# Five edits in a two-block transformer kernel: a 31-tap convolution from ScalarE and GpSimd to TensorE, row sums inverted small, heads in banks of one kind, the scan's two sums in one bank, and the inverse moved ahead

## The chip, the cores and the metric

The kernel runs on one core of one Trainium2 chip. The metric is the device time of one execution in microseconds (us). The engines go by the names of the profile: PE (TensorE), DVE (VectorE), ACT (ScalarE), POOL (GpSimd), SP (the queue that issues most weight DMAs). L12 is line 12 of the kernel before.

## What is computed

Two chained blocks, each of two layers, for 256 tokens of width 1024 in float32 (block one also carries 256 context tokens, so its even layer works on 512). Block one, layer 0: a bidirectional gated delta-rule scan (GDN, 8 heads of 64, chunks of 64 tokens) beside a latent attention (MLA, 8 heads). Layer 1: neighbourhood attention (NA) beside grouped attention (GQA), 8 heads each. Block two, in both layers: an attention over the 256 best keys of an indexer, a 31-tap depthwise convolution and a pooling, side by side. After each mixer stands an FFN. The parts that are changed:

```
# delta rule, one chunk                          # softmax attention
v_new = u - w @ s                                p = exp(s - max);  o = (p @ v) / sum(p)
o     = q_dec @ s + qk @ v_new                   # block two, convolution branch
s     = s * g_last + k_dec^T @ v_new             c[t] = sum_j y[t - 30 + j] * dw[j] + b   (31 taps)
u, w  from the inverse of (I + m), 64 x 64       z = layer_norm(c) -> silu -> @ pw
```

## The kernel before

All matmuls with weights are written as three products of parts (`mm3`, L549 to L551): the weight is cut into a high part (ACT cast, L270) and a low rest (a subtraction on DVE, in some stretches on POOL, L272), the activation likewise (`split`, L306 and L307). Weights come in tiles of 128 rows by up to 1024 columns over SP's queue. The program is recorded through a scheduler that orders the instructions of each engine by itself; the source order and the pools decide what it may choose from. PSUM has eight banks of 128x512 float32; `bank(K, kind)` takes the next of a kind, and the kinds are shared out per stage (in layer 0: "g" 3, "s" 2, "tp", "po", "gv" one each, and "aux" means "g" there; elsewhere there are two "s", two "acc", two "tp").

*Layer 0* (`l0_mixer`): the in-projections with a 5-tap convolution as products with diagonal matrices (`gdn_conv`: ACT makes a diagonal from the identity in L882, PE multiplies by it in L886); `gdn_norm` and `gdn_matrices` (L1040 multiplies chunks 64x64); `gdn_blocks`, an elimination of 31 steps on DVE (L1086, L1088); `gdn_invert`, which turns its result (L1105) and multiplies 32x32 blocks (L1115, L1128); then the scan `gdn_run`, whose step is `gdn_state`: L1188 gives w @ s in one half of the partitions and q_dec @ s in the other, L1195 gives the update of s, L1206 the product qk @ v_new, and `gdn_o` adds each of the last two sums to the output. `l0_mla` fills the gaps of the scan. `mod_chunk` makes the modulation (L372 to L400) from its own weights; chunks 4 and 5 are gates.

*Attention* (`attend`, and `s_attend` in block two): scores in two banks for two heads, maximum (L669), exponential with its sum (L671), transposes (L674), copies (L677, L679), p @ v (L685). The inverse sums come from `sums_row`: a reciprocal that DVE takes of the sum repeated over 64 columns of each head (L693), and a product with the identity that turns them (L695); `attended` multiplies (L713, L714).

*Block two* (`s_mixer`): in-projection weights, 1872 columns; the indexer's scores (L1596 on) and its selection of 256 keys (L1603 to L1623, DVE, with MAX8 and MATCH_REPLACE8); the convolution (`conv`): for each of 2 x 128 channels and each of 30 further taps

```
            nc.scalar.mul(m, yp[:, c, j:j + 256], dw[:, i, c, j:j + 1])
            nc.gpsimd.tensor_tensor(o, o, m, op=ALU.add)
```

(L1516 and L1517), its transposes (L1531), and its layer norm in `finish`; then `att(1)`, `att(0)` (scores L1638 and L1642, transposes L1653, copies L1654, p @ v L1659), and the out-projection.

## Time and profile before

| | us |
|---|---|
| median of 3 runs | 2181.03 (2169.08 to 2183.77) |
| the profiled execution | 2178.34, of it the span of the trace 2176.6 |
| PE busy | 1992.6 (92% of the span) |
| DVE / ACT / POOL busy | 1382.2 / 931.8 / 370.7 |
| mean granted clock of PE | 0.917 of full speed |

A busy PE is not a PE at full speed: its clock has two levels, 1.2 and 2.4 GHz, shown as 0.50 and 1.00. A stretch is therefore read by two numbers, how much of it PE was busy and at what clock.

### The profile page before, as it was taken

The numbers are of one execution on the slowest core, as the hardware profiler recorded it, in microseconds if no ns is written. First come the engines' busy times: TensorE is split into PE (matmuls) and PEld (weight loads), VectorE is DVE, ScalarE is ACT, GpSimd is POOL, SyncE is SP. The second block draws the span as 40 slices with busy tenths as digits, with TensorE's granted clock in tenths as the row PEclk, the third lists the DMA queues.
The fourth block names the chain that finished last, engine by engine and source line by source line (L and its number), as shares of the span: only waits on it lengthen the run. The fifth ranks groups of instructions, "written<-read, shape, count | busy, mean of one in ns | idle before, by whom it ended". The sixth has DMA issues, their size and how long they took to land.

```text
span 2176.6 us, 30043 instructions
## 1 busy us (share of the span) xinstructions
PE 1992.6 (92%) x11008; PEld 1585.0 (73%) x11008; DVE 1382.2 (64%) x2699; ACT 931.8 (43%) x1612; POOL 370.7 (17%) x454
## 2 busy tenths in 40 slices
PE   6989799898999999899879998988899998879998
PEld 4778578678878778676557887865688787558886
DVE  5665557767776744638575555785765568666644
ACT  4533443344222234444454443753554357345532
POOL 2211112301000000213130002641200057040000
PEclk9999799899999999999788999966999999579999
DMA  8344540233676632223044573513556443055652
GB/s 279 90 112 122 190 131 26 67 98 111 191 259 215 189 106 93 90 68 97 20 145 141 164 230 100 145 54 113 168 175 195 153 113 109 29 164 166 191 186 68
DMA packets 186947, 291.82 MB, mean 134 GB/s; under 512 B 28472, under 2 KB 75704, under 8 KB 186800
## 3 DMA queue, kind: packets, MB, share of 16 engines
q1 hardware_dynamic: 172720, 272.54, 40.2%
q0 software_dynamic: 5472, 16.13, 2.3%
q10 hardware_dynamic: 8608, 1.23, 0.4%
q8 instruction: 87, 1.43, 0.3%
q14 instruction: 60, 0.49, 0.1%
HBM read 281.44 MB, written 8.41 MB: 133 GB/s over the span
## 4 chain that ended last, share of the span: by engine, by line
PE 75%; DVE 13%; DMA 5%; ACT 4%; issue 2%; POOL 1%; SPq 0%; ACTq 0%; DVEq 0%; POOLq 0%
PE acc L549 17%; PE acc L550 17%; PE acc L551 17%; DVE wlo L272 2%; DMA wraw<-in_w_in_dram 2%; PE s L549 2%; PE s L550 2%; PE s L551 2%; PE po L685 2%; PE tp L886 2%; DMA wraw<-in_w_mod_dram 1%; PE gv L372 1%; ACT whi L270 1%; PE tp L674 1%; PE s L1642 1%
## 5 line engine op out<-in xcount | busy, mean ns | idle before, releaser
L272 DVE TENSOR_TENSOR wlo<-wraw,whi 128x512 fp32r<-128x512 f32 (+4 forms) x748 | 488.7, 697 | 292.4 <-ACT whi L270 276.5
L270 ACT CAST whi<-wraw 128x1024 fp32r<-128x1024 f32 (+4 forms) x420 | 413.4, 989 | 456.1 <-PE acc L551 180.9
L549 PE MATMUL acc<-whi,u 128*128 128x512 f32 (+3 forms) x1320 | 512.5, 391 | 28.3 <-ACT u L306 15.9
L550 PE MATMUL acc<-wlo,u 128*128 128x512 f32 (+3 forms) x1320 | 511.7, 389 | 4.4 <-DVE wlo L272 4.4
L551 PE MATMUL acc<-whi,u 128*128 128x512 f32 (+3 forms) x1320 | 510.3, 388 | 0.8 <-DVE u L307 0.7
L549 PEld LDWEIGHTS acc<-whi,u 128*128 128x128 f32 x1320 | 254.3, 193 | 80.9 <-ACT u L306 18.2
L550 PEld LDWEIGHTS acc<-wlo,u 128*128 128x128 f32 x1320 | 254.3, 193 | 55.2 <-DVE wlo L272 8.0
L551 PEld LDWEIGHTS acc<-whi,u 128*128 128x128 f32 x1320 | 253.2, 192 | 52.3 <-DVE u L307 4.3
L272 POOL TENSOR_TENSOR wlo<-wraw,whi 128x512 fp32r<-128x512 f32 (+1 forms) x92 | 115.1, 1280 | 400.5 <-ACT whi L270 400.4
L549 PE MATMUL acc<-u,whi 128*128 128x512 f32 (+1 forms) x480 | 174.1, 369 | 5.0 <-ACT u L1558 2.7
L550 PE MATMUL acc<-u,whi 128*128 128x512 f32 (+1 forms) x480 | 174.0, 364 | 2.4 <-DVE u L307 2.4
L551 PE MATMUL acc<-u,wlo 128*128 128x512 f32 (+1 forms) x480 | 173.1, 365 | 2.2 <-DVE wlo L272 2.2
L1517 POOL TENSOR_TENSOR u<-u,cvm 128x256 f32<-128x256 f32 x120 | 100.3, 836 | 64.2 <-ACT cvm L1516 55.8
L549 PEld LDWEIGHTS acc<-u,whi 128*128 128x128 f32 x480 | 93.9, 197 | 21.6 <-ACT u L1558 3.1
L431 DVE SCALAR_TENSOR_TENSOR msum<-mraw,u,msum 128x512 f32<-128x512 f32 x140 | 100.8, 746 | 13.4 <-DMA mraw<-in_w_mod_dram 12.4
L550 PEld LDWEIGHTS acc<-u,whi 128*128 128x128 f32 x480 | 94.5, 197 | 17.7 <-DVE u L307 3.1
L551 PEld LDWEIGHTS acc<-u,wlo 128*128 128x128 f32 x480 | 94.1, 197 | 17.6 <-DVE wlo L272 2.8
L307 DVE TENSOR_TENSOR u<-aux,u 128x512 fp32r<-128x512 f32 (+2 forms) x92 | 56.8, 629 | 34.8 <-ACT u L306 34.4
L306 ACT CAST u<-aux 128x512 fp32r<-128x512 f32 (+2 forms) x92 | 48.5, 541 | 59.2 <-PE aux L724 25.9
L549 PE MATMUL acc<-whi,dxh 128*128 128x512 f32 x176 | 69.7, 396 | 1.9 <-ACT dxh L306 1.9
L550 PE MATMUL acc<-wlo,dxh 128*128 128x512 f32 x176 | 69.6, 395 | 0.0
L551 PE MATMUL acc<-whi,dxl 128*128 128x512 f32 x176 | 69.0, 396 | 0.0
(501 smaller groups left out, 3037.8 us busy)
## 6 DMA issues: line engine op xcount, KB each, us to landing
wraw<-in_w_up_dram SPq DMA_DIRECT2D x64, 512.0 KB, 3.9
wraw<-in_w_down_dram SPq DMA_DIRECT2D x64, 512.0 KB, 4.2
mraw<-in_w_mod_dram SPq DMA_DIRECT2D x56, 512.0 KB, 4.9
wraw<-in_w_ffn_down_dram SPq DMA_DIRECT2D x44, 512.0 KB, 3.7
wraw<-in_w_mod_dram SPq DMA_DIRECT2D x40, 512.0 KB, 5.4
wraw<-in_w_ffn_gate_dram SPq DMA_DIRECT2D x48, 256.0 KB, 3.5
wraw<-in_w_ffn_up_dram SPq DMA_DIRECT2D x48, 256.0 KB, 3.9
wraw<-in_w_ffn_gate_dram SPq DMA_DIRECT2D x20, 512.0 KB, 3.8
```

Source lines behind the costliest of these rows:

```text
L270: self.K.nc.scalar.copy(hi, raw)
L272: e.tensor_tensor(lo[:, k], raw[:, k], hi.bitcast(F32)[:, k], op=ALU.subtract)
L306: (hi_eng or nc.scalar.copy)(hi, src)
L307: nc.vector.tensor_tensor(lo, src, hi.bitcast(F32), op=ALU.subtract)
L372: nc.tensor.matmul(ps[32 * j:32 * j + 32, :], K.cl[:, g + k, :], raw[:, k, :], start=(g + k < 4), stop=(g + k >= 4))
L431: nc.vector.scalar_tensor_tensor(accs[s], raw[:, k, :], c, accs[s], op0=ALU.mult, op1=ALU.add)
L549: mm(ps, ah, bh, start=start, stop=False)
L550: mm(ps, ah, bl, start=False, stop=False)
L551: mm(ps, al, bh, start=False, stop=stop)
L685: nc.tensor.matmul(po[hh * 64:hh * 64 + 64, c:c + 128], v(hh, j), pts[hh][0][:, j * 128:(j + 1) * 128], start=(j == 0), stop=(j == nj - 1))
L886: nc.tensor.matmul(tp[:, t * 128:(t + 1) * 128], x[:, t // 2, t % 2 * 128 + j:t % 2 * 128 + j + 128], dg[j], start=(j == 0), stop=(j == 4))
L1517: nc.gpsimd.tensor_tensor(o, o, m, op=ALU.add)
```

## The change

1. **Convolution.** The 240 ACT and POOL instructions of both layers go. ACT now makes a 128x128 diagonal per tap (`taps`, 32 per half of the channels, the 32nd being the bias against a tile of ones), and PE multiplies the shifted input by it, 64 products into each of the banks "po" and "tp" per layer and half of the channels taken together, so that the sum over taps is formed in PSUM. The transposes of L1531 go; `finish` reads the two banks.
2. **Sums.** `sums_row` goes. A reciprocal is taken of the sums alone (2 or 4 columns), and `normed` spreads four pairs at once (one DVE copy of 128x512), turns them with four products, copies and multiplies.
3. **Banks.** In layer 1, pairs take ("s","s","tp","tp") and ("acc","acc","tp","tp") in turn; in block two the second group of heads takes "acc". The transposes kept in `late` are recorded ahead of `na(1)`.
4. **Scan.** L1188 becomes two products of 64 columns; the q_dec @ s half stays open, and qk @ v_new is added to it in the same bank. One `gdn_o` per step instead of two, one bank less.
5. **Order in layer 0.** `gdn_invert` stands right behind `gdn_blocks`; `gdn_norm(0)` and `gdn_matrices(True)` stand ahead of the second convolution group and the gate projection; modulation chunks 4 and 5 stand in the middle of `l0_mla`.

```
-def sums_row(K, sm, rb, c):
-    n = sm.shape[1]
-    r = cut(K, [128, n, 2, 64], F32, "rs%d" % n, 2)
-    K.nc.vector.reciprocal(r, bc(sm, [128, n, 2, 64], 3))
-    for x in range(n):
-        K.nc.tensor.matmul(rb[:, c + x * 128:c + x * 128 + 128], r[:, x]..., K.ident, ...
+def normed(K, y, po, R, kind):
+    rb = bank(K, kind)
+    w = cut(K, [128, 512], F32, "pt", K.np)
+    K.nc.vector.tensor_copy(w..., bc(R.rearrange("p x h -> p (x h)"), [128, 8, 64], 2))
+    for x in range(4):
+        K.nc.tensor.matmul(rb[:, x * 128:x * 128 + 128], w[:, x * 128:x * 128 + 128], K.ident, ...
+    K.nc.scalar.copy(y, rb)
+    K.nc.vector.tensor_tensor(y, po, y, op=ALU.mult)
...
-            nc.tensor.matmul(ps[:, p * 128:(p + 1) * 128], wq[:, p, 2 * a:2 * a + 2, :]..., S[:, p, :], start=True, stop=True)
+            nc.tensor.matmul(ps[r, c], wq[:, p, 3 * a, :], S[:, p, :], start=True, stop=True)
+            nc.tensor.matmul(ps[o, c], wq[:, p, 1 + a, :], S[:, p, :], start=(p == 0), stop=False)
...
-        nc.tensor.matmul(po[o, hs], Q[r, h, :], vn[r, hs], start=True, stop=True)
-    if not first:
-        gdn_o(K, t, a, o, ps)
+        nc.tensor.matmul(po[o, hs], Q[r, h, :], vn[r, hs], start=first, stop=first or h == 7)
     gdn_o(K, t, a, o, po)
...
+    def taps(c):
+        for j in range(32):
+            if j % 3 == 0:
+                dg = cut(K, [128, 3, 128], F32, "dg", 2)
+            nc.scalar.mul(dg[:, j % 3, :], K.ident, dw[:, i, c, j:j + 1] if j < 31 else dwb[:, i, c:c + 1])
+            yield j, dg[:, j % 3, :]
+    def conv():
+        ps = [bank(K, "po"), bank(K, "tp")]
+        for c in range(2):
+            for j, dg in taps(c):
+                for t in range(2):
+                    nc.tensor.matmul(ps[t][:, c * 128:c * 128 + 128],
+                                     yp[:, c, t * 128 + j:t * 128 + j + 128] if j < 31 else ones, dg, ...
+        return ps
...
-    pss = [bank(K, "s") for _ in range(2)]
+    pss = [bank(K, "acc" if g else "s") for _ in range(2)]
...
-                        LX = gdn_blocks(K, Om)
+                        gdn_invert(K, *gdn_blocks(K, Om))
...
+                        gdn_norm(K, 0)
+                        gdn_matrices(K, True)
+                        with On(K, pg):
                             gdn_conv(K, W, 8, 4, False, True)
                             gdn_gate(K, W)
-                        gdn_norm(K, 0)
-                        gdn_matrices(K, True)
```

What the scheduler makes of it is seen in PE's order. Layer 0, before: the products of the inverse (L1115, L1128) stand behind the last pieces of `gdn_matrices` (L1040) and between modulation products (L372), with the scan's first products (L1154) next.

```order
L1040 MATMUL g_1901<-gT_1899,gT_1892 64x64 x8
L1040 MATMUL g_1902<-gT_1899,gT_1892 64x64 x8
L1115 MATMUL g_2013<-b_2009,u_144 32x32 x32
L1115 MATMUL g_2048<-b_2009,u_144 32x32 x32
L372 MATMUL gv_3272<-wraw_3273,u_124 32x512 x2
L372 MATMUL gv_3272<-wraw_3277,u_124 32x512 x2
L1128 MATMUL g_2083<-u_144,b_2010 32x32 x32
```

Layer 0, now (these lines are L1121 and L1134, `gdn_matrices` is L1034 and L1046):

```order
L1034 MATMUL tp_1796<-const_id_75,u_138 128x128 x4
L1121 MATMUL g_1136<-b_1132,u_144 32x32
L1121 MATMUL g_1171<-b_1132,u_144 32x32
L1121 MATMUL g_1136<-b_1132,u_144 32x32 x31
L1121 MATMUL g_1171<-b_1132,u_144 32x32 x31
L1134 MATMUL g_1206<-u_144,b_1133 32x32 x32
L1034 MATMUL tp_1803<-const_id_75,u_137 128x128
```

The inverse stands between the pieces of `gdn_matrices` now (row 591 of PE's order, where it stood at 750); the second convolution group and the gate projection follow it, and the scan's first state comes at row 798.

Block two, first layer, behind the last product of the in-projection; before: the indexer's products (L549 to L551 into "s") and turned queries (L1345), then the attention scores (L1638).

```order
L549 MATMUL s_12879<-u_12042,u_12120 128x128
L550 MATMUL s_12879<-u_12043,u_12120 128x128
L551 MATMUL s_12879<-u_12042,u_12121 128x128
L1345 MATMUL aux_12607<-const_id_75,akd_12593 128x128 x2
L1345 MATMUL aux_12612<-const_id_75,u_11693 128x128 x4
L1638 LDWEIGHTS u_11664
L1638 MATMUL s_12984<-u_11697,u_11664 128x256
```

Now (L1352 was L1345, L1648 was L1638, L1534 is the new product of the convolution):

```order
L550 MATMUL s_12868<-u_12064,u_12092 128x128
L551 MATMUL s_12868<-u_12063,u_12093 128x128
L1352 MATMUL aux_12616<-const_id_75,akd_12606 128x128 x2
L549 MATMUL s_12868<-u_12063,u_12099 128x128
L1534 MATMUL po_12640<-dg_12672,u_11719 128x128
L1534 MATMUL tp_12641<-dg_12672,u_11719 128x128
```

The convolution's products come in groups of up to twelve (two tiles of three diagonals) between the indexer's products and the attention scores: 10 of the layer's 128 stand ahead of the last product of the in-projection, 118 behind it, and the last of them ahead of the first p @ v.

## Rows read from the trace of the kernel before

**Rows 1.** The page: busy time, share of the span and instructions of each engine; PE's granted clock in tenths in 40 slices of 54.4 us; and the chain that ended last, by engine.

```profile
PE 1992.6 (92%) x11008; PEld 1585.0 (73%) x11008; DVE 1382.2 (64%) x2699; ACT 931.8 (43%) x1612; POOL 370.7 (17%) x454
...
PEclk9999799899999999999788999966999999579999
...
PE 75%; DVE 13%; DMA 5%; ACT 4%; issue 2%; POOL 1%; SPq 0%; ACTq 0%; DVEq 0%; POOLq 0%
```

**Rows 2.** Layer 0, stretches of time: start and end, length, busy time (and instructions) of PE, its weight loads, DVE, ACT and POOL, granted clock of PE, share of the DMA engines, GB/s.

```profile
142.00:200.00 58.00, 58.00 (x363) 49.94 (x365) 45.21 (x91) 20.62 (x45) 2.56 (x2) 1.00 0.26 73
200.00:220.00 20.00, 18.04 (x102) 14.05 (x94) 5.62 (x6) 5.93 (x11) 4.43 (x4) 1.00 0.59 123
220.00:240.00 20.00, 12.85 (x175) 6.54 (x174) 6.32 (x15) 4.91 (x9) 3.34 (x5) 0.83 0.66 208
240.00:260.00 20.00, 16.68 (x416) 10.88 (x414) 15.46 (x69) 10.88 (x29) 5.33 (x21) 0.57 0.64 217
260.00:280.00 20.00, 19.36 (x270) 16.09 (x267) 10.18 (x28) 9.41 (x17) 1.39 (x3) 0.66 0.34 108
280.00:390.00 110.00, 105.03 (x1194) 83.22 (x1192) 72.92 (x128) 44.08 (x104) 21.31 (x30) 1.00 0.24 75
```

**Rows 3.** Layer 0, DVE in order of time (start, duration, line, operation, out<-in, shape, and in brackets the idle time before it and who ended it): the last step of the elimination, and the second half of the turning that follows it.

```profile
191.43 0.22 DVE L1088 TENSOR_TENSOR u<-u,b 128x62 f32<-128x62 f32 x1
...
201.30 1.24 DVE L1105 STREAM_TRANSPOSE b<-u 32x1024 f32<-32x1024 f32 x1 [0.51 <-DMA u<-scx]
```

**Rows 4.** Layer 0, from the chain of waits in order of time (start, duration, what): the two longest transfers on it between 200 and 280.

```profile
225.66 7.09 DMA wraw<-in_w_mod_dram
...
239.47 5.38 DMA mrow<-in_b_mod_dram
```

**Rows 5.** Layer 1's mixer, stretches of time, columns as in rows 2.

```profile
1010.00:1030.00 20.00, 17.27 (x111) 11.28 (x109) 19.47 (x59) 8.00 (x17) 11.91 (x22) 0.95 0.20 60
1030.00:1050.00 20.00, 17.05 (x105) 11.68 (x103) 13.62 (x34) 9.38 (x20) 6.84 (x7) 0.71 0.09 34
1050.00:1070.00 20.00, 14.13 (x43) 8.01 (x44) 8.98 (x15) 6.50 (x16) 0.00 (x0) 0.55 0.09 27
1070.00:1090.00 20.00, 20.00 (x130) 13.53 (x128) 11.05 (x16) 8.92 (x22) 0.00 (x0) 0.86 0.00 1
1090.00:1107.00 17.00, 13.24 (x105) 9.32 (x104) 11.33 (x18) 8.81 (x19) 0.00 (x0) 0.98 0.10 32
```

**Rows 6.** Layer 1's mixer, 1010 to 1107, the longest of who waited for whom (total, times, longest).

```profile
ACT p L671 <- DVE nmx L669: 24.7, 14, 3.7
```

**Rows 7.** The reciprocals of block one's attentions (L693): count, shortest/median/longest in ns, first and last start, shape.

```profile
L693 DVE RECIPROCAL rs<-sm x32: 935/953/954, 311.9 to 1099.8; 128x128 f32<-128x128 f32 x32
```

**Rows 8.** Block two, first layer's mixer, stretches of time, columns as in rows 2. The last product of the in-projection starts at 1431.7, the first of the out-projection at 1502.5.

```profile
1350.00:1360.00 10.00, 8.08 (x52) 7.67 (x53) 4.78 (x10) 2.92 (x5) 2.51 (x6) 0.72 0.46 136
1360.00:1410.00 50.00, 45.67 (x291) 42.83 (x291) 35.97 (x68) 38.92 (x85) 33.16 (x41) 0.97 0.51 142
1410.00:1434.00 24.00, 20.92 (x130) 18.93 (x129) 23.83 (x39) 16.80 (x36) 20.62 (x25) 1.00 0.38 111
1434.00:1450.00 16.00, 10.63 (x50) 8.39 (x50) 16.00 (x53) 6.82 (x18) 6.05 (x8) 0.50 0.13 34
1450.00:1490.00 40.00, 36.00 (x126) 22.22 (x126) 21.03 (x65) 11.75 (x41) 0.00 (x0) 0.50 0.09 26
1490.00:1503.00 13.00, 8.46 (x28) 4.66 (x26) 7.32 (x9) 4.52 (x8) 1.14 (x2) 0.50 0.09 34
```

**Rows 9.** The same layer, DVE in order of time, columns as in rows 3: the cut of 128x512 weights while POOL runs L1517 and after its last one.

```profile
1434.78 1.24 DVE L272 TENSOR_TENSOR wlo<-wraw,whi 128x512 fp32r<-128x512 f32 x1
...
1436.34 0.67 DVE L272 TENSOR_TENSOR wlo<-wraw,whi 128x512 fp32r<-128x512 f32 x1
```

**Rows 10.** The same layer, PE in order of time, columns as in rows 3.

```profile
1437.27 0.69 PE L1345 MATMUL aux<-const_id,akd 128*128 128x128 f32 x2 [5.30 <-DVE akd L1696]
...
1502.54 0.80 PE L549 MATMUL acc<-whi,u 128*128 128x512 f32 x1 [2.45 <-ACT whi L270]
```

**Rows 11.** The out-projection, from 3.5 us behind its first product, columns as in rows 2.

```profile
1506.00:1508.00 2.00, 2.00 (x11) 1.59 (x10) 0.22 (x1) 0.00 (x0) 0.00 (x0) 1.00 0.86 242
```

**Rows 12.** The convolution's two instructions, and the diagonals of layer 0's 5-tap convolution, columns as in rows 7.

```profile
L1516 ACT ACTIVATE cvm<-u,u x120: 494/507/550, 1363.5 to 1860.1; 128x256 f32<-128x256 f32 x120
...
L1517 POOL TENSOR_TENSOR u<-u,cvm x120: 722/804/1097, 1364.0 to 1860.9; 128x256 f32<-128x256 f32 x120
...
L882 ACT ACTIVATE cvo<-const_id,u x32: 385/388/403, 88.9 to 183.6; 128x128 f32<-128x128 f32 x32
```

**Rows 13.** Layer 0's 5-tap products, PE in order of time, columns as in rows 3 (two records to a product).

```profile
190.24 1.05 PE L886 MATMUL tp<-cvo,u 128*128 128x128 f32 x8
191.12 0.39 PE L886 MATMUL tp<-cdg,u 128*128 128x128 f32 x2
```

**Rows 14.** The scan, PE in order of time, columns as in rows 3 (two records to a product).

```profile
366.74 1.06 PE L1188 MATMUL g<-u,gwq 128*128 128x128 f32 x8
367.63 0.60 PE L674 MATMUL tp<-const_id,p 128*128 128x128 f32 x4
...
370.73 1.09 PE L685 MATMUL po<-pt,u 128*64 128x128 f32 x14
371.74 0.33 PE L674 MATMUL tp<-const_id,p 128*128 128x128 f32 x1
```

More of the change, by code (lines that the diff above doesn't have):

```diff
@@ L656, in heads_T, with attend @@
     feat_split(K, hi, lo, ps[:, :T * 128], scale)
-def attend(K, score, v, po, rb, c, kinds=("s", "s", "tp", "tp")):
+def attend(K, score, v, po, R, x, kinds=("s", "s", "tp", "tp")):
     nc = K.nc
@@ L706, in pair_scores, with attended @@
     return [ps[:, :n] for ps in pss]
-def attended(K, po, rb, hi, lo, k0, t):
-    n = po.shape[-1] // 128
-    y = cut(K, [128, 512], F32, "pt", K.np)[:, :n * 128]
-    K.nc.scalar.copy(y, rb)
-    K.nc.vector.tensor_tensor(y, po, y, op=ALU.mult)
+def attended(K, po, R, hi, lo, k0, t):
+    y = cut(K, [128, 512], F32, "p", K.np)
+    normed(K, y, po, R, "aux")
     tk = slice(t * 128, (t + 1) * 128)
-    split(K, hi[:, k0:k0 + n, tk], lo[:, k0:k0 + n, tk], y.rearrange("p (k t) -> p k t", k=n))
+    split(K, hi[:, k0:k0 + 4, tk], lo[:, k0:k0 + 4, tk], y.rearrange("p (k t) -> p k t", k=4))
 def out_features(K, O, hi, lo, k0, t):
@@ L834, in l0_mla @@
     for pair in range(4):
+        if pair == 2:
+            gates()
         heads = {}
@@ L854, in l0_mla @@
             heads[h] = (q1, q2, k1, k2)
-        po, rb = bank(K, "po"), bank(K, "gv")
+        po, R = bank(K, "po"), inverse_sums(K)
         for t in range(4):
@@ L864, in score @@
                     yield pss[hh][:, :n]
-            attend(K, score, lambda hh, j: vt[:, j, pair * 128 + hh * 64:pair * 128 + hh * 64 + 64], po, rb, t * 128,
+            attend(K, score, lambda hh, j: vt[:, j, pair * 128 + hh * 64:pair * 128 + hh * 64 + 64], po, R, t,
                    ("s", "g", "tp", "g") if late else ("s", "s", "tp", "tp"))
-        nc.scalar.copy(O[:, pair, :], rb)
-        nc.vector.tensor_tensor(O[:, pair, :], po, O[:, pair, :], op=ALU.mult)
+        normed(K, O[:, pair, :], po, R, "gv")
 def gdn_conv(K, W, f0, nf, silu, tensor):
@@ L1032, in gdn_matrices @@
         kT, xT = qk[0], qk[-1]
-        kk = [aux(K), aux(K)]
+        kk = [bank(K, "gv"), bank(K, "po")] if second else [aux(K), aux(K)]
         for p in range(4):
@@ L1394, in na @@
     def na(t):
-        po, rb = bank(K, "po"), aux(K)
+        po, R = bank(K, "po"), inverse_sums(K)
         for pair in range(4):
@@ L1403, in score @@
                 return out
-            attend(K, score, lambda hh, j: vn[:, j, pair * 128 + hh * 64:pair * 128 + hh * 64 + 64], po, rb, pair * 128,
-                   ("s", "acc", "tp", "acc") if t == 1 and pair >= 1 else ("s", "s", "tp", "tp"))
-        attended(K, po, rb, oh, ol, 0, t)
+            attend(K, score, lambda hh, j: vn[:, j, pair * 128 + hh * 64:pair * 128 + hh * 64 + 64], po, R, pair,
+                   ("acc", "acc", "tp", "tp") if t == 1 and pair % 2 else ("s", "s", "tp", "tp"))
+        attended(K, po, R, oh, ol, 0, t)
     def gqa(t):
-        po, rb = bank(K, "po"), aux(K)
+        po, R = bank(K, "po"), inverse_sums(K)
         for pair in range(4):
@@ L1414, in score @@
                 return pair_scores(K, (gqh[:, pair], gql[:, pair]), (gkh[:, g], gkl[:, g]), 512, tok(t), pss)
-            attend(K, score, lambda hh, j: vg[:, j, g * 64:g * 64 + 64], po, rb, pair * 128, ("s", "acc", "tp", "acc"))
-        attended(K, po, rb, oh, ol, 4, t)
+            attend(K, score, lambda hh, j: vg[:, j, g * 64:g * 64 + 64], po, R, pair,
+                   ("acc", "acc", "tp", "tp") if pair % 2 else ("s", "s", "tp", "tp"))
+        attended(K, po, R, oh, ol, 4, t)
     linear_tok(K, W, xs, w, chunks, [(2, 0), (2, 1), (2, 2), (2, 3), (1, 0), (1, 1), (1, 2), (1, 3), (0, 2), (0, 3)],
@@ L1476, in s_conv @@
     nc.gpsimd.memset(up[:, :, 0:16], 0.0)
-    cv, px = cut(K, [128, 2, 256]), cut(K, [128, 2, 256])
+    px = cut(K, [128, 2, 256])
+    ones = cut(K, [128, 128])
+    nc.gpsimd.memset(ones, 1.0)
     pw = cut(K, [128, 2, 256])
@@ L1683, in att @@
     def att(t):
-        po, rb = bank(K, "po"), aux(K)
+        po, R = bank(K, "po"), inverse_sums(K)
         for g in range(2):
-            s_attend(K, g, t, qh, ql, kh, kl, mask[t], U, po, rb)
-        attended(K, po, rb, oh, ol, 0, t)
+            s_attend(K, g, t, qh, ql, kh, kl, mask[t], U, po, R)
+        attended(K, po, R, oh, ol, 0, t)
     def qkv():
@@ L1847, in l0_mixer @@
                 K.O = sbt(K, [128, 4, 512], pool=K.po)
-                with On(K, g2):
-                    gdn_invert(K, *LX)
                 closed(K, g2)
@@ L1854, in l0_mixer @@
                     with Pool(K, "mla", "right"):
-                        for n in range(4, 10):
-                            mod_chunk(K, W, K.po, 0, n)
-                        l0_mla(K, Om)
+                        for n in range(6, 10):
+                            mod_chunk(K, W, K.cur, 0, n)
+                        l0_mla(K, Om, lambda: [mod_chunk(K, W, K.cur, 0, n) for n in (4, 5)])
 def layer0(K):
```

57 lines of the change are left out of this document (22 added, 35 removed).

## The prediction

> **What bounds the kernel now.** I read the page first. PE is busy 92% of the span and 75% of the chain that ended last is PE, so time is saved only where PE idles or runs slowly [rows 1]. The clock row of the same page shows where that is: the slices with a 6, 5 or 7 lie in layer 0's mixer, in layer 1's mixer and in block two's two mixers. The projections between them stand at 9. All five edits work in those mixers, so I cut the four stretches finer and asked of each how much PE work it holds, counted at full speed (busy time times granted clock), and what PE waited for.
>
> - Layer 0, 200 to 280: 18.0 + 12.85 x 0.83 + 16.68 x 0.57 + 19.36 x 0.66 = 51 us of work in 80 us, so 29 us are lost [rows 2]. From 280 to 390 PE is busy 105 of 110 us at 1.00; there nothing but less PE work helps.
> - Layer 1, 1010 to 1107: 16.4 + 12.1 + 7.8 + 17.2 + 13.0 = 66.5 us of work in 97 us, so 30.5 us are lost [rows 5]. The longest wait is that of the exponential for the maximum, 24.7 us in 14 times [rows 6].
> - Block two's mixer, first layer (the second has the same shape): up to 1434, 5.8 + 44.3 + 20.9 = 71 us of work in 84, 13 us lost; DVE is busy 23.83 of the last 24 us. From 1434 to 1503 PE is busy 10.63 + 36.00 + 8.46 = 55.1 of 69 us, all at 0.50, which is 27.5 us of work [rows 8]. This begins with 5.30 us in which PE waits for DVE [rows 10].
>
> **The inverse moved ahead (layer 0).** It removes nothing; it changes what PE does while DVE eliminates and turns. The elimination ends at 191.65, the turning, which waits for a transfer, at 202.5 [rows 3]. Until now the second convolution group and the gate projection filled that time (they end near 220), and behind them a chain stood uncovered: operands, modulation with transfers of 7.09 and 5.38 us [rows 4], the products of the inverse, the state. Now PE meets the inverse at about 190 and waits until 202.5, some 12 us, since what was recorded behind it stands behind it in PE's queue; after that some 30 us of dense work cover the chain's rest, and chunks 4 and 5 with their transfers on SP's and POOL's queues come later, inside the MLA. Of 29 us lost about 14 stay: **-15 us**. If the wait is covered by the pieces of the matrices, -25; if SP's weights for the moved projection come late behind it, or the chunks then stop the MLA, +5.
>
> **Banks and sums (layer 1).** Pairs that take two score banks of one kind in turn let PE make the scores of the next pair while the last one is in its exponential, and DVE loses 16 reciprocals of 0.953 us [rows 7], 15 us of its 64 in this stretch [rows 5], against four copies of some 0.7. The work is the same 66.5 us. Both bounds are set by the 30.5 us lost: nothing, if the transposes, which now share two banks for all pairs, are what holds; -20, if most pairs overlap. I take about a quarter, **-8 us**, since only one of several waits goes. In the MLA the other 16 reciprocals lie beside a full PE: nothing. If that cover were thin they would be worth the 5 us in which PE idles there.
>
> **The scan.** PE's work per step stays unless the halves fail to run side by side. One step's four products of 128 columns take 0.89 us (366.74 to 367.63). Seven products of 64 columns in alternate halves took 1.01 us (370.73 to 371.74), some 0.13 us each with the entry into that form [rows 14], so eight need 1.05 to 1.15. With 14 steps that have a state this is **+3 us** (0 to +4), and it counts because PE is full there. Fourteen fewer additions on DVE and a bank more buy nothing beside a full PE.
>
> The Trainium skill (TensorEngine Tiling (Array Packing), Tiling Modes) says that independent tiles run in parallel, but also that a change of tiling mode drains the engine; it gives no time for a drain. The rows just named show the entry at about 0.1 us, so by the rule with the trace's size the term stays +3; a drain that undid the overlap is the fourth rival.
>
> **The convolution (block two, twice).** Out go 60 ACT multiplications of 0.507 us and 60 POOL additions of 0.804 us per layer; in come 64 diagonals on ACT (the same operation took 0.388 us, so 25 us against 30) [rows 12] and 128 products on PE. Four of this form take 0.88 us [rows 13], so one 0.22 and the layer's 128 some 28 us at full clock, 56 at half.
>
> *Up to 1434.* POOL's additions slow DVE: the same weight cut takes 1.24 us while one runs and 0.67 behind the last [rows 9]. With POOL silent DVE, which is late there, gains; ACT loses some 27 of its multiplications. Ten products (2.2 us) join. Of 13 us lost I take back half: **-6 us** (-11 to +2).
>
> *Behind 1434.* The work is 27.5 + 118 x 0.22 = 53.5 us at full clock, 107 at half, in a stretch that took 69. The waits of PE there were 69 - 55.1 = 13.9 us; the 5.30 us of [rows 10] is filled by convolution, which leaves 8.6. The layer norm, which had lain beside attention products, now begins only when the sum is complete, and "po" is held until it has read it, so p @ v starts after it: some 4.5 us more (an estimate: two statistics and a dozen DVE operations of a few columns, each under the 0.67 us of [rows 9]). At full clock throughout 53.5 + 8.6 + 4.5 = 66.6; with the tail still at half clock (scores of the second group, p @ v, transposes and turned sums, which I count as 29 of the 55.1 us), 14.5 more, 81. What will the clock be? In 1450 to 1490 PE was busy 36 of 40 us and stayed at 0.50 [rows 8], so being busy was not enough there. But layer 0's stretch from 142 to 200, full of exactly these 128x128 products among projections, stood at 1.00 [rows 2, 13], and within 3.5 us of the out-projection's first product the clock was up [rows 11]. The convolution's groups make up half of PE's time there, so I expect full clock up to the end of the convolution and a part of the tail at half: 71 us, **+2 us** (-3 to +12, and up to +50 if the clock never rises).
>
> Per layer -6 + 2 = -4, both **-8 us**.
>
> **Sum.** -15 - 8 + 3 - 8 = -28 us. The profiled execution took 2178.3, 2.7 below the median of the runs and inside their spread, so I work from it: 2150.
>
> **Rivals.**
> 1. *The convolution's products run at half clock* (slower). For it: PE at 0.50 through 40 us of nearly unbroken products [rows 8]. Against it: the same form at 1.00 in layer 0 [rows 2]. Price: behind 1434 some 107 + 13 = 120 us for 69, +45 with the relief ahead of it, twice. 2178 - 15 - 8 + 3 + 90 = 2248; if the clock rises half way through, 2178 - 20 + 2 x 18 = 2194. It decides from a stretch of about 85 us on, where the other terms are used up.
> 2. *Nothing is left.* DVE's relief meets a PE that is full at 0.97 to 1.00 for most of 1360 to 1434 [rows 8], PE waits at the inverse, the transposes' two banks hold layer 1: -5 + 0 + 3 + 2 x 2 = +2, 2180.
> 3. *More comes back.* The matrices cover the inverse (-25), most pairs overlap (-15), and in block two -11 and -3 per layer: -25 - 15 + 3 - 28 = -65, 2113. For it: DVE full at twice the duration in the last 24 us ahead of 1434 [rows 8, 9]. Against it: the weights' transfers and ACT's casts are late there too.
> 4. *The scan's halves run one after another*: eight times 0.22 is 1.78 us for 0.89, 14 steps +12.5 instead of +3: 2160. Against it stand the seven products in 1.01 us [rows 14]. The drain named in the sentence on the skill above would act here.
>
> **Chances.** Forecast 0.42, rival 1 0.15, rival 2 0.17, rival 3 0.19, rival 4 0.07. A measurement of this kernel can tell about 1% (22 us) from no change. Faster by over 1%, below 2159: nine tenths of the forecast, all of rival 3, half of rival 4, 0.61. Within 1%: the rest of these, rival 2 and a little of rival 1, 0.26. Slower: 0.13. The range reaches from below rival 3 to the half-way case of rival 1, 2103 to 2198; the forecast's own is 2130 to 2170.
>
> **What would show it.** Right: 200 to 260 at a clock near 1.00 but for one wait at the inverse of about 12 us, with the scan starting 15 to 20 us earlier; block two's weight cuts before 1434 no longer than half of what they take now, per column the 0.67 us of [rows 9]; the convolution's products 0.22 us apart; last in-projection product to out-projection 66 to 81 us; the scan's eight products in about 1.1 us. Wrong: convolution products 0.44 us apart; PE waiting for diagonals from ACT (64 x 0.388 us against 28 us of products is near balance, and ACT's exponentials stand in the same queue); a wait at the inverse over 20 us; layer 1's stretch still 92 to 97 us.

## The result and the profile after

| | us |
|---|---|
| median before, 8 runs | 2170.26 (2166.74 to 2183.77) |
| median after, 8 runs | 2192.58 (2186.68 to 2196.81) |
| ratio, 95% interval | 1.0082 [1.0058, 1.0106] |
| the profiled execution after | 2186.68, of it the span 2184.9 |

I forecast 28 us less; it became 22 us more. The page of after, the lines that answer to [rows 1]:

```profile
PE 2012.9 (92%) x11624; PEld 1618.5 (74%) x11624; DVE 1305.7 (60%) x2697; ACT 920.2 (42%) x1616; POOL 272.6 (12%) x336
...
PEclk9996889999999999999798999997999999879999
...
PE 83%; DVE 8%; ACT 4%; DMA 2%; issue 2%; POOL 0%; SPq 0%; ACTq 0%; DVEq 0%; POOLq 0%
```

DVE and POOL lost the work that was to go, the mean clock rose from 0.917 to 0.938, and still the time grew: a 6 and two 8s stand early in the clock row. To place it I took the start of the same projection product in both traces, stage by stage. The first product of the projection behind layer 0's mixer starts at 449.9 before and 464.4 after: **+14.5** (forecast -15, with the scan's +3 -12). Layer 1's mixer, from the last projection product ahead of it to the first behind it, takes 89.6 and 88.4: -1.2 (-8). In block two the in-projections, first product to last, are 7.9 and 11.7 shorter (-6 each); the tails, from the last in-projection product to the first of the out-projection, are 6.6 and 7.6 longer (+2 each). The rest is under +1, which leaves +8.3 between the two profiled executions. The medians lie 22.3 apart, because before's profiled execution was 8.1 above the median of its 8 runs and after's 5.9 below: all terms were sized on one of the longer executions of before.

Two readings of mine ahead of the prediction were wrong. The 1431.7 of [rows 8] is a product of the indexer's scores; the last in-projection product starts at 1430.5, and tails are counted from there (72.0 us before, where 1431.7 gives 70.8). And the 31 steps of the elimination on DVE stand in `gdn_invert`, ahead of its turning, not in `gdn_blocks`: part 5 moves them too, though the scheduler has them on DVE at about the same time in both kernels (142.9 to 191.7 before, 143.6 to 190.8 after).

**Layer 0.** Stretches of after, columns as in [rows 2]:

```profile
160.00:180.00 20.00, 15.72 (x89) 13.14 (x87) 16.91 (x30) 9.41 (x16) 0.00 (x0) 0.99 0.21 58
180.00:200.00 20.00, 5.43 (x77) 4.05 (x77) 12.87 (x34) 2.70 (x4) 4.62 (x4) 0.50 0.56 131
200.00:220.00 20.00, 18.01 (x534) 16.36 (x530) 5.33 (x8) 9.32 (x16) 0.00 (x0) 0.50 0.52 105
220.00:240.00 20.00, 17.45 (x141) 14.49 (x137) 4.81 (x11) 4.88 (x11) 0.00 (x0) 0.73 0.49 159
240.00:260.00 20.00, 20.00 (x181) 17.00 (x180) 2.58 (x4) 4.34 (x12) 0.00 (x0) 1.00 0.16 53
260.00:280.00 20.00, 18.33 (x121) 15.27 (x122) 4.30 (x7) 6.21 (x11) 5.64 (x4) 0.96 0.11 41
280.00:300.00 20.00, 16.67 (x152) 13.10 (x148) 16.07 (x78) 8.33 (x27) 6.21 (x23) 0.59 0.34 107
```

Busy time times clock gives 40 us of work in the 80 us from 160 to 240. [Rows 2] had 58 of 58 up to 200. PE in order of time, the rows with the long waits, and the first of the inverse:

```profile
186.83 1.09 PE L1034 MATMUL tp<-const_id,u 128*128 128x128 f32 x4 [11.11 <-DVE u L951]
...
192.47 1.08 PE L1034 MATMUL tp<-const_id,u 128*128 128x128 f32 x4 [1.70 <-ACT gT L1036]
198.92 0.37 PE L1046 MATMUL gv<-gT,gT 64*64 64x64 f32 x1 [5.36 <-ACT gT L1036]
...
201.97 3.46 PE L1121 MATMUL g<-b,u 32*32 32x32 f32 x121 [0.53 <-DVE b L1111]
```

The last projection product started at 175.3. From there PE stands, not at the inverse but at the next transposes of `gdn_matrices` (L1034), which wait for the norm. DVE in order of time shows what the norm shares it with:

```profile
185.16 2.98 DVE L951 TENSOR_TENSOR u<-u,rsy 128x512 f32<-128x512 f32 x2
...
190.54 0.23 DVE L1094 TENSOR_TENSOR u<-u,b 128x62 f32<-128x62 f32 x1
...
198.97 1.23 DVE L1111 STREAM_TRANSPOSE b<-u 32x1024 f32<-32x1024 f32 x1 [6.89 <-DMA u<-scx]
200.68 1.24 DVE L1111 STREAM_TRANSPOSE b<-u 32x1024 f32<-32x1024 f32 x1 [0.47 <-DMA u<-scx]
```

The norm's multiplication (L951) comes between steps of the elimination (L1094), which ends at 190.8 as it ended at 191.7 before [rows 3], and the turning behind it at 201.9 (before: 202.5). The small steps that lead up to the multiplication, eleven DVE operations, take 8.4 us (176.49 to 184.86) between the elimination's. The third wait, 5.36 us, is not DVE's: PE waits for a copy by ACT (L1036), and ACT first issues the inverse's own transfers:

```profile
193.46 4.78 ACTq L1102 DMA_DIRECT2D u<-scx  x4
198.28 0.59 ACT L1036 COPY gT<-tp 128x512 f32<-128x512 f32 x1 [5.95 <-issue]
```

So the inverse holds up the matrices as well as itself, and what PE had to do in the meantime now stands behind both. After the stop the inverse's 32x32 products (from 201.97) run at 0.50; the second convolution group and the gate projection follow at 1.00 and 0.96 from 240 to 280, when what they used to cover is over.

**Layer 1.** Who waited for whom, 1024 to 1121 (total, times, longest), for [rows 6]:

```profile
ACT pt L679 <- PE po L686: 13.4, 8, 2.8
ACT p L702 <- PE aux L700: 12.1, 4, 4.5
DVE pt L677 <- PE tp L674: 11.9, 11, 1.8
```

The exponential's 24.7 us in 14 times have become 3.3 in one; copies that wait for p @ v, for the turned sums (L700, `normed`) and for the transposes stand at the head instead. PE stands idle as long as before, 15.0 us of 89.6 and 16.0 of 88.5: the wait that the forecast named went, and others took its place.

**Block two, first layer.** Stretches, for [rows 8]; the last in-projection product now starts at 1433.9, the first of the out-projection at 1512.5:

```profile
1410.00:1434.00 24.00, 24.00 (x158) 22.62 (x157) 23.25 (x47) 12.67 (x24) 9.33 (x12) 1.00 0.38 113
1434.00:1450.00 16.00, 16.00 (x142) 15.04 (x140) 9.84 (x38) 10.44 (x32) 0.00 (x0) 1.00 0.12 34
1450.00:1470.00 20.00, 19.75 (x164) 16.95 (x163) 11.42 (x42) 14.66 (x44) 0.00 (x0) 1.00 0.09 27
1470.00:1480.00 10.00, 6.40 (x53) 5.80 (x55) 4.45 (x18) 1.68 (x5) 0.00 (x0) 1.00 0.00 1
1480.00:1490.00 10.00, 9.24 (x34) 5.44 (x33) 3.61 (x8) 2.25 (x8) 0.00 (x0) 0.50 0.15 45
1490.00:1500.00 10.00, 10.00 (x32) 6.39 (x32) 2.38 (x7) 1.66 (x6) 0.00 (x0) 0.50 0.02 9
```

PE in order of time, for [rows 10, 13]:

```profile
1475.29 0.39 PE L1534 MATMUL po<-dg,u 128*128 128x128 f32 x2
1475.52 0.39 PE L1534 MATMUL tp<-dg,u 128*128 128x128 f32 x2
1479.50 0.44 PE L1553 MATMUL acc<-const_id,lnx 128*128 128x128 f32 x2 [3.60 <-DVE lnx L1550]
...
1512.53 0.49 PE L549 MATMUL acc<-whi,u 128*128 128x512 f32 x1 [3.05 <-ACT whi L270]
```

The convolution runs at 1.00, 0.22 us a product, as priced (each of these rows is one product, two records). Behind its last product PE waits 3.60 us for the layer norm, and the tail goes on at 0.50 for 20 us. The diagonals (L1525, columns as in [rows 7], then who waited for them, us and times) hold PE hardly at all:

```profile
L1525 ACT ACTIVATE dg<-const_id,u x128: 384/387/412, 1365.6 to 1885.2; 128x128 f32<-128x128 f32 x128
...
  PEld po L1534: 1.3, 3
```

The weight cuts on DVE by shape, 1405 to 1434 (count, then total us and mean ns), before and after:

```profile
L272 DVE TENSOR_TENSOR wlo<-wraw,whi 128x384 fp32r<-128x384 f32 x14 | 11.7, 894 | 0.0
```
```profile
L272 DVE TENSOR_TENSOR wlo<-wraw,whi 128x384 fp32r<-128x384 f32 x16 | 10.9, 733 | 2.0 <-ACT whi L270 2.0
...
L272 DVE TENSOR_TENSOR wlo<-wraw,whi 128x512 fp32r<-128x512 f32 x2 | 1.3, 684 | 0.0
```

The 128x512 cut is at the 0.67 us that [rows 9] had behind POOL's last addition; the other shape fell by a fifth, not by half.

**The scan.** One step's eight products (two lines, each row one record of two to a product), for [rows 14]:

```profile
385.51 0.32 PE L1196 MATMUL g<-u,gwq 128*64 128x128 f32 x1
385.52 0.32 PE L1197 MATMUL g<-u,gwq 128*64 128x128 f32 x1
...
386.54 0.44 PE L674 MATMUL tp<-const_id,p 128*128 128x128 f32 x2
```

1.03 us to the next product, where [rows 14] has 0.89: 14 steps make +2.

### The profile page after: what moved, and what is told of

It is laid out like the page before. It is cut to its first block, busy times and chain, and to the rows that moved or that the text cites. A ratio compares the mean times of both kernels' runs of the same rounds, so it can differ in the third digit from the quotient of the medians.

```text
span 2184.9 us, 31041 instructions
## 1 busy us (share of the span) xinstructions
PE 2012.9 (92%) x11624; PEld 1618.5 (74%) x11624; DVE 1305.7 (60%) x2697; ACT 920.2 (42%) x1616; POOL 272.6 (12%) x336
## 4 chain that ended last, share of the span: by engine, by line
PE 83%; DVE 8%; ACT 4%; DMA 2%; issue 2%; POOL 0%; SPq 0%; ACTq 0%; DVEq 0%; POOLq 0%
PE acc L549 19%; PE acc L551 18%; PE acc L550 18%; PE s L549 2%; PE s L551 2%; PE s L550 2%; PE tp L892 2%; PE po L686 2%; PE tp L674 1%; PE gv L372 1%; PE po L1534 1%; PE tp L1534 1%; DMA wraw<-in_w_mod_dram 1%; PE aux L729 1%; DVE u L539 1%
## 5 line engine op out<-in xcount | busy, mean ns | idle before, releaser
L272 DVE TENSOR_TENSOR wlo<-wraw,whi 128x512 fp32r<-128x512 f32 (+4 forms) x748 | 466.7, 667 | 298.9 <-ACT whi L270 282.7
L549 PE MATMUL acc<-whi,u 128*128 128x512 f32 (+3 forms) x1320 | 512.5, 391 | 28.8 <-ACT u L306 16.3
L551 PE MATMUL acc<-whi,u 128*128 128x512 f32 (+3 forms) x1320 | 510.5, 388 | 3.1 <-DVE u L307 3.1
L549 PEld LDWEIGHTS acc<-whi,u 128*128 128x128 f32 x1320 | 253.8, 192 | 79.2 <-ACT u L306 18.7
L551 PEld LDWEIGHTS acc<-whi,u 128*128 128x128 f32 x1320 | 253.6, 192 | 54.3 <-DVE u L307 6.1
L549 PE MATMUL acc<-u,whi 128*128 128x512 f32 (+1 forms) x480 | 171.9, 365 | 2.2 <-ACT u L306 2.1
L551 PE MATMUL acc<-u,wlo 128*128 128x512 f32 (+1 forms) x480 | 171.3, 362 | 0.0
L549 PEld LDWEIGHTS acc<-u,whi 128*128 128x128 f32 x480 | 92.2, 194 | 17.8 <-ACT u L306 3.1
L551 PEld LDWEIGHTS acc<-u,wlo 128*128 128x128 f32 x480 | 92.6, 194 | 15.3 <-issue 1.7
L549 PE MATMUL acc<-whi,dxh 128*128 128x512 f32 x176 | 69.7, 396 | 1.9 <-ACT dxh L306 1.9
L551 PE MATMUL acc<-whi,dxl 128*128 128x512 f32 x176 | 69.0, 396 | 0.0
L532 DVE TENSOR_TENSOR y<-acc,u 128x512 f32<-128x512 f32 x40 | 27.4, 688 | 56.8 <-ACT yj L531 56.7
```

The lines of the kernel that those rows point to most:

```text
L272: e.tensor_tensor(lo[:, k], raw[:, k], hi.bitcast(F32)[:, k], op=ALU.subtract)
L532: nc.vector.tensor_tensor(y[:, cs], ps, G(t)[:, cs], op=ALU.mult)
L549: mm(ps, ah, bh, start=start, stop=False)
L551: mm(ps, al, bh, start=False, stop=stop)
```

## The experiments

Ratios are to the kernel before in executions beside each run, with 95% intervals. "Layer 0" is the start of the first projection product behind its mixer; "tail" and "layer 1" are as above. These three columns come from one profiled execution each. Some expectations name other marks of the same places: a start of 460.5 before and 474.8 after is a product some 10.5 us further on.

| run | median us | ratio | layer 0 | layer 1 | tails |
|---|---|---|---|---|---|
| before (stages: the execution of 2178.34) | 2170.26 | | 449.9 | 89.6 | 72.0, 71.1 |
| after | 2192.58 | 1.0082 [1.0058, 1.0106] | 464.4 | 88.4 | 78.6, 78.7 |
| e1_old_order | 2174.69 | 1.0005 [0.9986, 1.0024] | 453.4 | 90.4 | 75.1, 77.7 |
| e2_order_alone | 2195.64 | 1.0101 [1.0047, 1.0155] | 471.7 | 92.0 | 66.1, 69.2 |
| e4_between | 2174.08 | 1.0000 [0.9978, 1.0023] | 449.9 | 90.2 | 78.5, 77.7 |
| e5_half_elim | 2177.38, one run | | 452.0 | 88.6 | 78.7, 78.4 |
| e9_scan_alone | 2178.14 | 1.0025 [0.9991, 1.0059] | 449.3 | 99.8 | 70.8, 65.7 |
| e3_conv_alone | 2166.88 | 0.9968 [0.9946, 0.9990] | 450.4 | 99.8 | 73.4, 73.7 |
| e12_banks_sums | 2159.22 | 0.9930 [0.9904, 0.9956] | 446.2 | 88.5 | 58.2, 58.5 |
| e16_conv_banks | 2168.32 | 0.9991 [0.9967, 1.0015] | 451.5 | 88.3 | 75.1, 77.8 |
| e10_no_taps | 2134.57, one run | | 443.3 | 89.7 | 61.6, 58.2 |
| e13_before_again | 2161.82, one run | | 445.0 | 92.5 | 66.1, 64.6 |
| e8_fill | 2161.11 | 0.9950 [0.9927, 0.9974] | 449.7 | 90.5 | 73.3, 73.4 |
| e11_cover | 2157.99 | 0.9920 [0.9896, 0.9944] | 452.0 | 90.2 | 72.7, 70.9 |
| e14_cover_ge | 2142.73 | 0.9855 [0.9832, 0.9878] | 438.6 | 90.2 | 72.6, 72.4 |
| e15_no_conv | 2144.18 | 0.9875 [0.9847, 0.9903] | 441.5 | 88.5 | 61.2, 60.4 |
| e17_no_conv_scan | 2152.73 | 0.9907 [0.9878, 0.9936] | 444.1 | 88.4 | 61.6, 60.8 |

**The order in layer 0.** Undone in after (e1), and made alone in before (e2, the same edit the other way round); the edit is condensed:

```
-    gdn_invert(K, *gdn_blocks(K, Om))
+    LX = gdn_blocks(K, Om)
     ...
-    gdn_norm(K, 0); gdn_matrices(K, True)      # these go behind gdn_gate
     gdn_conv(K, W, 8, 4, False, True); gdn_gate(K, W)
+    gdn_norm(K, 0); gdn_matrices(K, True)
     ...
+    gdn_invert(K, *LX)                         # chunks 4 and 5 ahead of l0_mla, kk in "aux" again
```

> The changed kernel with layer 0's order as before (part 5 undone, chunks 4 and 5 and the two banks of the second matrices with it). In the changed kernel the first projection product behind layer 0's mixer came 14.4 us later than before. Theory (order): the normalisation and the matrices, put ahead of the second convolution group, wait for DVE, whose queue is full with the elimination, so PE idled 160 to 240; undone, the first projection product is back within 3 us of its 460.5 us of before, and the whole is 12 to 20 us below the changed kernel. Rival (scan): the split products and the shared bank of the scan are slow; then the stretch stays 8 us or more late. Rival (sums): the pairs' common tail in the MLA is late; the same.

> The kernel before with part 5 alone (layer 0's order, its chunks and its two banks). Theory (order): slower than before by 12 to 18 us, the first projection product at 472 to 478 us. Rivals (scan, sums): within 4 us of before.

e2 alone costs 1.0%, 24 us of median, and its layer 0 ends 21.8 us later than before's, both more than the 12 to 18 expected; e1 takes 0.8% off after, and its layer 0 ends 11.0 us earlier, 3.5 behind before. Part 5 is the loss: without it the other four come out at 1.0005. Stretches of e2, where the hole has the shape of after's:

```profile
180.00:200.00 20.00, 6.35 (x80) 4.75 (x80) 12.37 (x33) 2.70 (x4) 4.62 (x4) 0.50 0.60 127
200.00:220.00 20.00, 18.15 (x550) 16.54 (x550) 4.89 (x7) 10.15 (x18) 0.00 (x0) 0.50 0.44 97
```

Two runs ask whether it is missing cover for DVE. In e4 only the second convolution group goes back ahead of the norm; in e5 DVE's elimination is made shorter by every second step.

```
+    gdn_conv(K, W, 8, 4, False, True)          # e4
     gdn_norm(K, 0); gdn_matrices(K, True)
-    gdn_conv(K, W, 8, 4, False, True)
     gdn_gate(K, W)

-    for j in range(31):                        # e5, gdn_invert
+    for j in range(0, 31, 2):
```

> The changed kernel with one move: the second convolution group stands ahead of the normalisation and the matrices again, the gate projection stays behind them; the inverse stays early. Theory (order): PE is busy at full clock until about 205 us, the inverse and the matrices fall among the gate's products, and the first projection product comes 20 to 30 us earlier than in the changed kernel, so below before's 460 us. Rival (the inverse's own transfers and small products at half clock cost the time wherever they stand): 5 us or less against the changed kernel.

> The changed kernel with every second of the 31 elimination steps left out (the output changes): DVE's elimination, some 35 us of work in the 47 us up to 190.8, is halved, everything else stands. Theory (DVE's queue is what PE waits for): the wait of 11.1 us for the normalised q and the one for the inverse shorten, the first projection product comes 10 to 18 us earlier than the changed kernel's 474.8. Rival (transfers: the weights of the second group and the inverse's round trip through memory): less than 5 us earlier.

e5: layer 0 ends 12.4 us earlier, inside the range, but not by the mechanism expected. DVE in order of time, the last step of its elimination and the norm's multiplication:

```profile
165.61 0.22 DVE L1094 TENSOR_TENSOR u<-u,b 128x62 f32<-128x62 f32 x1
...
188.59 2.14 DVE L951 TENSOR_TENSOR u<-u,rsy 128x512 f32<-128x512 f32 x2
```

The elimination is over 25 us earlier than in after, and the norm comes 3.4 us later (the whole run is 3.9 later at layer 0's first norm). Its eleven small steps take 2.4 us instead of 8.4, but begin only at 186.13. What closes the hole is the inverse: its products start at 178.2 and stand where PE had waited. That the elimination alone delays the norm is therefore not shown; that its result comes too late for PE is. e4: 14.4 us earlier, against 20 to 30 expected, and PE is full where it stood, so the hole was missing cover; the chunks and the matrices' banks that part 5 moved as well stay moved in e4 and are not the loss. Against e1, the same parts in the old order, layer 0 ends 3.5 us earlier, which two executions of before differ by as well (e13): that the early inverse gains once it is covered is not shown. The rest is in the rows behind it: stretches of e4, and from its waits from 200 to 280 those on the decay factors "gE".

```profile
180.00:200.00 20.00, 19.87 (x128) 17.32 (x127) 12.98 (x28) 5.23 (x10) 2.56 (x2) 1.00 0.62 159
...
240.00:260.00 20.00, 10.56 (x158) 6.81 (x155) 8.39 (x34) 6.30 (x24) 5.60 (x22) 0.67 0.65 209
```
```profile
DVE gQ L1057 <- DMA gE<-Ed: 11.8, 5, 3.8
...
PE gv L1046 <- DVE gQ L1057: 3.7, 1, 3.7
...
PE gv L372 <- DVE gQ L1057: 3.6, 1, 3.6
```

DVE waits for "gE", a load with two tiles, five times. It waited for it before as well (9.2 us in four times) and in after (7.0 in three); that PE now waits for DVE's result is new. e14 (below) gives the load five tiles.

**The scan alone** (`gdn_state` of after in before):

> The kernel before with part 4 alone (the scan's step). Theory (halves side by side): the eight products take 1.0 to 1.2 us per step against 0.89, first projection product behind the mixer 0 to 5 us later than before. Rival (one after another, or a drain at each change of form): 1.7 us or more per step, 10 us or more later.

A step's eight products take 1.02 us, layer 0 ends 0.6 us earlier, and the ratio is not told from 1. The fourth rival falls.

**Convolution, banks and sums, apart and together.** e3 is before with part 1, e12 before with parts 2 and 3, e16 with 1 to 3. e10 is before with `na = 1` for `na = 31` in its `conv` and the DVE branch behind it off, so that 30 of 31 taps are left out, for what the relief of ACT, POOL and DVE is worth at most.

> The kernel before with part 1 alone (the convolution's products). Block two's first mixer: theory (the convolution itself gives and takes): 6 to 8 us gained up to the last in-projection product, because POOL's additions no longer slow DVE, and 5 to 8 us given back between it and the out-projection, because 28 us of products stand there, the layer norm idles PE for 3 to 4 us and the tail then runs at 0.50. Whole: within 6 us of before. Rival (banks and sums of parts 2 and 3 are what makes the tail late): the gain stays and the tail takes no longer than the 70.8 us of before; whole 12 to 18 us faster.

> The kernel before with the 30 further taps of the convolution left out (one tap and the bias stay; the output changes): neither ACT, POOL nor PE has them. Theory (POOL slows DVE, and DVE is what the in-projection waits for): up to the last in-projection product 6 to 9 us are gained, as in the changed kernel, and the stretch behind it, without the 5.3 us wait, takes 60 to 68 us of its 70.8. Rival (ACT's multiplications, not POOL, hold the in-projection): the two-input DVE operations keep their double durations.

> The kernel before with parts 2 and 3 alone (small sums, heads in banks of one kind). Layer 1's mixer, last product ahead to first product behind it, took 88.4 to 90.5 us in five traces with these parts and 89.6, 92.0, 99.8, 99.8, 89.7 in five without. Theory (they take the long case away): 87 to 91 us. Rival (they do nothing, the traces differ by chance): anything from 88 to 100. Layer 0: theory (the common tail of four pairs costs the MLA) 2 to 4 us later than before; rival (the scan costs it) 0 to 1. Whole: between 8 us faster than before and equal.

> The kernel before with parts 1, 2 and 3 (convolution, sums, banks); the scan and layer 0's order as before. Parts 2 and 3 alone were 15 us faster than before (tails of 58.2 and 58.5 us in block two), part 1 alone 7 us. Theory (the convolution on PE and the new banks fill the same idle PE, so the gains don't add): the tails take 74 to 79 us, the in-projection 7 us less, whole 0 to 8 us faster than before, no better than the convolution alone. Rival (the scan's step was what cost the sum): tails of 60 to 66, whole 18 to 25 us faster.

e10 has in-projections 7 and 13 shorter than before and tails 10 and 13 shorter; e3 has the same relief ahead of the tail (8 and 11) and pays in it (1 and 3, less than the 5 to 8 expected): alone the convolution on PE gains 0.3%. e12 gains 0.7%, more than the 8 us expected at most, and not where I looked: its tails are 13 shorter than in the first profile of before, in an execution (2148.75) that was the fastest of its four. The whole tail of its first layer as one stretch, columns as in [rows 2], in before, e12, after and (convolution and banks) e16:

```profile
1430.50:1502.50 72.00, 56.10 (x215) 36.05 (x213) 47.23 (x135) 25.54 (x74) 9.90 (x14) 0.52 0.09 26
```
```profile
1423.90:1482.10 58.20, 44.34 (x215) 28.63 (x213) 41.91 (x136) 23.60 (x71) 8.77 (x12) 0.74 0.13 43
```
```profile
1433.90:1512.50 78.60, 69.20 (x453) 53.74 (x451) 36.93 (x122) 37.41 (x117) 1.15 (x2) 0.87 0.10 30
```
```profile
1419.30:1494.40 75.10, 65.17 (x454) 51.33 (x452) 36.73 (x123) 37.47 (x117) 1.14 (x2) 0.93 0.10 32
```

Work is busy time times clock: 29 us of 72 before, 33 of 58 in e12, 60 of 79 in after, 61 of 75 in e16. Before lost 43 us there and e12 25. Of before's 43, 27 are clock and 16 idle time. PE stands idle nearly as long in e12 (13.9 us for 15.9), which gains by standing at 0.74 where before stood at 0.52; why its clock is higher is not shown. The convolution's 28 us were to lie in those 43; on top of the banks they meet 25, and the tail grows by 17 and 19 from e12 to e16. The in-projections give back 8 to 12 per layer in both. So the two gains, 0.3% and 0.7%, do not add: e16 is at 0.9991. What the sums took off DVE is seen in the reciprocals of block two, columns as in [rows 7], before and after.

```profile
L693 DVE RECIPROCAL rs<-asm x8: 1695/1743/1753, 1456.9 to 1908.6; 128x256 f32<-128x256 f32 x8
```
```profile
L1666 DVE RECIPROCAL rs<-asm x8: 168/177/178, 1466.9 to 1916.8; 128x4 f32<-128x4 f32 x8
```

How much of e12's gain is the sums and how much the banks was not tried, so that the reciprocals held the tail is not shown.

**Before again.** The kernel unchanged, to see what one profile is worth.

> The kernel before, profiled in another execution. Theory (the same instructions find PE's clock up at one time and down at another in the stretches full of small products): layer 1's mixer differs from the 89.6 us of the first trace, up to 100, with PE as busy and only the granted clock lower, or block two's tails differ from 72.0 and 71.1 us, down to 66; the big products between agree to 0.1 us. Rival (the stretches are fixed, and it was the other parts' code that moved them): all three stretches within 0.5 us of the first trace.

Its tails are 6 us shorter each than in the first profile, its layer 0 ends 4.8 earlier, layer 1 takes 2.9 longer. The stretches between differ by 0.4 to 2.4 us, not by the 0.1 expected.

**Versions.** e8: e4, with the convolution in the banks "acc" behind `att(1)`, and both groups' scores in "s". e11: the products ahead of `att(1)` and the layer norm between the two attentions. e14: e11 with five tiles of "gE". e15: e14 with the convolution back on ACT and POOL and the banks of part 3. e17: e15 with the scan of before.

```
-    ps = [bank(K, "po"), bank(K, "tp")]                        # e8
+    ps = [acc(K), acc(K)]
...
+    cv = conv(); ...; att(1); finish(cv); att(0)               # e11; e8 has conv() behind att(1)
...
-    e = cut(K, [128, 8, 64], F32, "gE", 2)                     # e14, gdn_matrices
+    e = cut(K, [128, 8, 64], F32, "gE", 5)
```

> The changed kernel with the second convolution group ahead of the matrices (as in the run before), the convolution in the two acc banks, its products recorded behind the first attention and their layer norm ahead of the second, both attentions' scores in the s banks. Theory (the tail is late because po is held until the layer norm has read it, and because nothing covers the layer norm): the convolution's products fill the waits of the attention, PE has no idle stretch over 2 us there, and last in-projection product to out-projection takes 60 to 70 us instead of 78; whole 10 to 30 us below before. Rival (28 us of products more is what costs): 74 us or more, whole within 6 us of before.

> As the run with the convolution in the two acc banks, but its products are recorded ahead of the first attention and its layer norm behind that one and ahead of the second. Theory (the layer norm's 3.7 us of idle PE and the clock that falls behind it are what is left of the tail): the products end some 10 us earlier, the layer norm lies beside products of the second attention, last in-projection product to out-projection takes 66 to 71 us instead of 73.3, whole 14 to 24 us below before. Rival (the products' own 28 us fill the stretch): 73 us or more.

> As the run named in the sentence on layer norm cover (convolution in acc, layer norm between the attentions, second convolution group ahead of the matrices), and five instead of two tiles for the decay factors that the matrices load back from memory. With two, DVE waited five times for them, 11.8 us in all, while PE had nothing else. Theory (that serial load is what is left of layer 0's uncovered stretch): first projection product 6 to 10 us earlier than with two tiles (456.0), whole 20 to 32 us below before. Rival (the next wait, the weights of the MLA, takes its place): 3 us or less.

> The best version so far (second convolution group ahead of the matrices, five tiles of decay factors, sums, banks, scan's step: 2143 us) with the 31-tap convolution taken back to ACT and POOL and block two's order of the mixer as before. Theory (28 us of products per layer cost more than POOL's slowing of DVE): in-projection 7 us longer per layer, tails 58 instead of 72.5, so 10 to 16 us faster than that version, 2127 to 2135. Rival (in the version with its layer norm covered the convolution on PE is worth its place): the same or slower, 2140 or more.

> The same, with the scan's step as before too (products of 128 columns, two additions per step). Theory (the split costs PE some 3 us in a stretch where PE is full): 1 to 5 us faster than the same with the new step. Rival (the freed bank and the additions are worth more): slower by 2 us or more.

e8 and e11 take 4 to 7 us off each tail of e4; at 73.3 and 73.4, 72.7 and 70.9 they stay above the 60 to 70 and, but for the last, the 66 to 71 expected. e14's layer 0 ends 13.4 earlier than e11's (expected: 6 to 10), and it is the best version, 1.45% under before. Five tiles in the order of before, which has the same waits, were not tried, so what the early inverse adds to them is open. e15 lies beside it, its interval overlapping, 9 us short of its forecast: tails 11 and 12 shorter, in-projections 8 to 11 longer. With its layer norm covered the convolution on PE is worth about what it costs. e17, expected faster than e15, has layer 0 end 2.6 later, and its ratio overlaps; that the new scan costs time is not borne out.

## Why the prediction was wrong

- **The inverse moved ahead** (-15, between -25 and +5; measured +14.5, alone +22). The failed step: "Now PE meets the inverse at about 190 and waits until 202.5, some 12 us". I followed PE's queue to the inverse's products and asked when their operand was ready, but not the same of `gdn_norm(0)` and `gdn_matrices(True)`, which I counted as work that fills time. They wait too, 11.1 us for the norm, which shares DVE with the elimination, and 5.4 us for ACT, which issues the inverse's transfers. Taking away the 30 us of dense work ahead of them stopped PE at 175.7 already; that, and the inverse at 0.50, cost 40 us of the 80 up to 240. My text even named that work as the cover of before. That the order is the loss is shown by e1 and e2, and that it is the missing cover by e4; e5 shows that the hole closes as well when the inverse comes sooner, not that the elimination delays the norm. A part came back: the stretch from 390 on, at 0.83 before, stands at 0.99 after (405 to 464).
- **Banks and sums, layer 1** (-8): -1.2 against the first profile. Six executions without parts 2 and 3 gave 89.6 to 99.8, mean 93.9; eleven with them 88.3 to 90.5, mean 89.3. So -4.6, mis-sized by nearly half, with the profile shown at the fast end; the one wait that I named went, and PE's idle time stayed.
- **Banks and sums, block two** (forecast nothing): with the convolution left alone, tails of 58.2 to 61.6 in three kernels against 64.6 to 72.0 in four executions of kernels without them, 8 us less per layer. I costed these parts only in layer 1 and put the tails at nothing, without asking what eight reciprocals of 1.743 us and one kind of score bank do there. Which of the two it was, and why the clock there is 0.69 to 0.74 with these parts and 0.52 to 0.62 without, is open.
- **The convolution.** Ahead of 1434: -6 per layer, measured -7.9 and -11.7; DVE's relief was real, though the 128x384 cuts fell by a fifth where I had named a half. Behind: +2, measured +6.6 and +7.6, in the range of -3 to +12. The products ran at full clock, the diagonals made PE wait 1.3 us in all, the layer norm took 3.6 of the 4.5 us priced, and the tail of 78.6 is inside the 66 to 81 named. The first rival is refuted. What the sum missed is that the slack it filled was the slack that the banks take. That the two layers' sum came out near the forecast, -5 for -8, is luck in part: both halves were larger than priced.
- **The scan** (+3): +2 by its rows (14 steps of 0.14), nothing measurable alone.

Had I given part 5 its loss and the rest as it was, the forecast would have been 2178 - 8 + 3 - 8 + 15 = 2180, inside 1%. The sum held one large term whose sign hung on a single reading of a queue.

The Trainium skill (TensorEngine Tiling (Array Packing), Tiling Modes) has a change of tiling mode drain the engine. The trace agrees as far as it goes: 1.03 us of a step against 0.89 leave 0.14 for a drain at most, and it does not show that a drain is what they are.

## What to carry to other kernels

Before a step is moved ahead in an in-order queue, ask of every instruction between its old and its new place when its operand is ready, and what independent work is left to stand in the hole; dense work that needs nothing belongs ahead of the work that waits. Two edits that fill the same lost time do not add, and together may gain less than the better one alone (0.1% here, for 0.3% and 0.7%), so count the loss once, as stretch less busy time times clock. And size a term of 1% on two profiles of the same kernel: stretches of the same instructions moved by 3 to 10 us here between executions.
